# Attention probabilities transposed on VectorE, value products in four 32-row strips of TensorE, in a fused encoder layer

## The chip, the cores and the metric

The program runs on one core of one Trainium2 chip. Its time is the device time of that core in microseconds. Shown are the median of three timed runs and one execution taken by the hardware profiler. TensorE (PE), VectorE (DVE), ScalarE (ACT), GpSimd (POOL) and SyncE (SP, which here only issues DMAs) each work through their own list of instructions in order, and wait for each other by semaphores.

## The reference

One encoder layer on x of 512 positions by 1024 channels, in float32:

```python
x = x + 0.5 * swiglu(rms_norm(x, ffn1_norm), ffn1_w_gate, ffn1_w_up, ffn1_w_down)   # D_FF = 2752
h = rms_norm(x, mix_norm)
u = h @ w_in                       # 512 Fourier | q 8x64 | k 2x64 | v 2x64
f_out = fourier_mixer(u[..., :512], fnet_w, fnet_b)      # 4 groups of 128
a_out = gqa_attention(...)         # per-head rms_norm of q and k, axial rotary, then for each head
    scores = q_blk @ k.T * 64**-0.5                      # 8 heads x 4 blocks of 128 queries, 512 keys
    p = jax.nn.softmax(scores, axis=-1); out = p @ v
x = x + concat([f_out, a_out]) @ w_out
x = x + 0.5 * swiglu(rms_norm(x, ffn2_norm), ...)
y = rms_norm(x, final_norm)
```

## The kernel before

The layer runs in three stretches: the first feed-forward block (to about 340 us), the mixer with the Fourier part, the attention and the output projection (about 340 to 497 us), and the second feed-forward block with the ending. The change is in the mixer. Numbers are kept to float32 accuracy by splitting each operand into a high part, rounded to the type fp32r that TensorE multiplies in one pass, and a low part, the rest; a product is then three products (`product`, L163 to L166: high by high, high by low, low by high), accumulated in a PSUM bank of 128 x 512 float32. The high part is a copy on ACT (or on DVE for the names in `HI_DVE`), the low part a subtraction on DVE (`lows`, L123).

The mixer's work is cut into named steps, each a small function put into the dictionary `ops`. A long table, `ORDER`, names them in the order in which they are recorded, and so fixes the order on every engine. The eight PSUM banks go round through a list: a step that writes takes the first spare bank (`bank_for`), the last step that reads it gives it back (`read`). The steps to follow are, for a pair of heads t (0 to 3), a key/value head b (0 or 1) and a block of 128 queries c (0 to 3):

- `n1.c`, `n1.m`, `n1.p`: column sums of squares of the mixer's input, and its reciprocal root r on GpSimd; `n1.t` and `n1.b` turn r into a row on PE and copy it. `k.s0`, `s1`, `s2` and the same for q0 to q3 make the scales of the heads, `sc`; `kw`, `kp`, `km` bring those of k onto k.
- `s` (L1188, L1189): the scores of 128 queries by 512 keys, two products of 512 columns.
- `m` (L1194, L1195): the row's maximum on DVE, then times the scale. `e` (L1202): the exponential on ACT, which also gives the row's sum z.
- `t` (L1214): for each block of 128 keys, four transposes of 128 x 128 on PE, which bring the probabilities of four query blocks into one bank, keys down the partitions. `h` (L1219) copies that bank to its high part `ph` on ACT, `l` subtracts it to `pl` on DVE.
- `v` (L1257): the value products. The 128 stationary columns in `vst` hold the high and the low part of v beside each other (64 + 64), so two products of 512 columns, by `ph` and by `pl`, do for a key block; after four key blocks `o.c` (ACT) and `o.a` (DVE) add the two halves of the bank.
- `z.r`, `z.w`, `z.p`, `r.m`, `r.h`, `r.l`: the division by z and the split of the result for the output projection `y0` to `y7` (24 products of 512 columns each).

So there are 32 steps of each of `s`, `m`, `e`, `t`, `h`, `l` and `v`: 128 transposes and 64 value products.

Of the kernel before, what the change touches and what calls it, by code (L numbers as in the profile page):

```python
# [37 lines left out]
HI_DVE = ("f0", "f1")  # L38
# [5 lines left out]
wk.r wq0.r wv.r cos wk.h wk.l wq0.h k.0 k.1 k.2 k.3 k.4 wv.h k.5 wq0.l k.6 wq1.r k.7 k.sq q0.0 wq1.h n1.c  # L44
k.rc n1.m k.sw n1.p q0.1 q0.2 q0.3 q0.4 wq1.l q0.5 wq2.r n1.t q0.6 q0.7 wq2.h q1.0 k.rs k.pq wv.l q0.sw
n1.b v.0 v.1 k.s0 k.s1 wq2.l q0.rc f2.r wq3.r q0.rs q0.ah q0.bh k.s2 v.2 kw v.3 v.4 v.5 v.6 q0.sq q0.al
q0.bl v.7 vt kp wq3.h km q1.1 wq3.l q0.pq f0.r q0.s0 k1.0 k0.0 k0.1 q1.2 q1.3 q1.4 q1.5 k1.2 k0.2 vp q1.6
q1.7 k0.3 s003 s001 s000 k1.1 k1.3 s010 f1.r v0.h v0.l q0.s1 q0.s2 f0.h m001 m003 s002 q1.sw m002 m010 q1.sq
q1.sd q1.pq e002 m000 v1.h e000 e001 e003 q2.0 q2.1 q2.2 q1.s0 q1.s1 f0.l q1.rc q1.rs v1.l q2.3 q2.4 q1.bh
q2.5 q2.6 q2.7 q2.sw t001 e010 f1.h f1.l q2.rc t000 q3.0 s012 h000 l000 s011 m011 t002 h002 h001 m012 q1.ah  # L50
q1.al q2.sq q3.1 q3.2 q3.3 q3.4 q3.5 q3.6 q1.bl q3.7 s013 l002 e011 v000 e012 f2.h l001 v001 q2.sd q3.sw
q2.rs t003 m013 q2.ah q3.rc q3.sq v002 e013 q2.bh f2.l s100 q1.s2 m100 s102 h003 q3.sd e100 f00.0 t010 f3.r
q2.bl h010 q2.pq l003 q2.s0 q2.s1 t013 m102 e102 s101 m101 f00.1 f00.u q2.al v003 l010 e101 t011 h011 q3.rs
s103 t012 f02.0 h013 l011 z0.r o00.c o00.a q3.bh v010 v011 m103 h012 l012 q3.pq q3.s0 l013 e103 s110 m110
s201 q3.ah s111 q3.bl v012 v013 o01.c t100 m111 h100 l100 e111 o0.r t101 h101 t102 h102 o01.a fw.r f02.1
e110 s112 m112 e112 z0.w pos q2.s2 l102 f01.0 s113 l101 z0.p m113 e113 s203 r0.m f02.e s200 m200 v100 v101
t103 t110 f01.1 r0.h h103 l103 z1.r f02.h v102 f01.u e200 q3.al q3.s1 v103 o10.c t112 m201 h110 r0.l h112
s202 m202 l110 t113 m203 f03.0 f03.1 v110 f3.h q3.s2 o10.a e201 s210 f03.e f3.l t111 l112 f10.0 f02.l h113
h111 l111 e202 f10.1 f03.h e203 s211 v111 m210 o2.r fw.h e210 t200 h200 t202 l113 m211 v112 s300 l200 v113
h202 t201 f10.u h201 l202 o11.c s212 m212 e212 s213 z1.w e211 f12.0 fw.l l201 f12.1 m300 e300 m213 e213  # L60
o11.a z1.p r1.m s301 v200 t203 r1.h f03.l h203 f12.e l203 f12.h z2.r z2.w v201 v202 t211 s302 m302 t210 h210
l210 s303 m303 h211 l211 v203 o20.c o20.a t212 h212 m301 f11.0 f13.0 e302 s311 l212 f12.l o0.h o0.l r1.l
t213 f11.1 f11.u m311 v210 v211 f13.1 h213 l213 f13.e e303 v212 s310 d00 m310 e301 t302 o1.r o1.h o1.l t301
f13.h f13.l e310 v213 o21.c t300 o21.a h302 l302 map0 map0.h map0.l d10 h300 l300 map1 z2.p d00.h map1.h
d00.l e311 t303 r2.m map1.l h303 l303 v300 s312 h301 m312 d20 d01 o2.h s313 d11 l301 v301 v302 v303 m313
e312 d01.h d01.l c0.s o2.l e313 t312 d11.h d11.l o30.c d31 o30.a h312 l312 o4.r c0.c c0.q c0.o t311 d10.h
# [1544 lines left out]
```

## Time and profile before

| | us |
|---|---|
| median of three runs | 838.54 (837.89 to 838.76) |
| the profiled execution's own time | 837.96 |
| its span, first to last instruction | 836.2 |
| PE busy | 829.4, 99% |
| DVE, ACT, POOL busy | 603.4, 461.9, 62.5 |

The span is 1.8 us shorter than the execution's own time, and that execution lies 0.6 us under the median. The busy time of PE is the union of matmuls that overlap one another: a matmul's duration holds its way through the array, and the next one starts long before it ends. What a matmul costs PE is therefore read from the distance between starts.

### The profile page before, as it was taken

To read this page: it belongs to the slowest core of one execution; us is meant where nothing else is said; L and a number is where in the kernel's file an instruction comes from. 1 tells how busy PE (TensorE), PEld (TensorE's weight loads), DVE (VectorE), ACT (ScalarE), POOL (GpSimd) and SP (SyncE) were. 2 spreads that over 40 slices of the span, in tenths; PEclk is the share of its full clock that TensorE was granted. 3 is DMA by queue.
4 is the path that set the end of the run, shared out by engine and by line. 5 is a ranking of instruction groups with operands and counts; after the bars stand their busy time and mean duration, and the time that the engine had idled before them with its cause. 6 is when DMAs were issued, how large, how long until landed. Compare 5 with 4: busy or idle time off the path is not lost.

```text
span 836.2 us, 13649 instructions
## 1 busy us (share of the span) xinstructions
PE 829.4 (99%) x5418; PEld 752.3 (90%) x5418; DVE 603.4 (72%) x923; ACT 461.9 (55%) x770; POOL 62.5 (7%) x69
## 2 busy tenths in 40 slices
PE   9999999999999999999999999999999999999997
PEld 7888998899989998889999888899988999899986
DVE  7977884578656867699999478878755885578563
ACT  7654763366434644677776446546533663356452
POOL 0111000000000000222000000110000000000001
PEclk9999999999999999999999999999999999999999
DMA  7787765468365423414020326777554674456122
GB/s 253 189 199 191 199 187 147 117 159 226 97 169 151 121 58 114 151 51 146 26 76 26 100 57 170 187 182 197 165 154 125 179 206 131 116 167 189 45 78 101
DMA packets 46110, 117.16 MB, mean 140 GB/s; under 512 B 5216, under 2 KB 9952, under 8 KB 45920
## 3 DMA queue, kind: packets, MB, share of 16 engines
q1 hardware_dynamic: 38128, 92.57, 33.5%
q0 software_dynamic: 7648, 23.47, 16.4%
q8 instruction: 42, 0.69, 0.3%
q10 hardware_dynamic: 272, 0.26, 0.1%
q14 instruction: 20, 0.16, 0.1%
HBM read 111.83 MB, written 2.10 MB: 136 GB/s over the span
## 4 chain that ended last, share of the span: by engine, by line
PE 99%; issue 0%; DVE 0%; POOLq 0%; POOL 0%; ACT 0%
PE r L429 23%; PE q L429 11%; PE dn L166 9%; PE dn L164 9%; PE dn L165 9%; PE p L429 6%; PE mix L164 4%; PE mix L166 3%; PE mix L165 3%; PE gu L766 3%; PE gu L164 3%; PE gu L165 3%; PE gu L166 3%; PE mix L1257 2%; PE mix L1214 2%; PE mix L1188 1%
## 5 line engine op out<-in xcount | busy, mean ns | idle before, releaser
L429 PE MATMUL r<-rt,ring 128*128 128x256 f32 x1686 | 204.9, 276 | 0.0
L429 PEld LDWEIGHTS r<-rt,ring 128*128 128x128 f32 x1686 | 198.5, 188 | 0.9
L165 PE MATMUL dn<-at,ring 128*128 128x512 f32 x295 | 114.8, 389 | 0.0
L166 PE MATMUL dn<-at,ring 128*128 128x512 f32 x295 | 114.8, 389 | 0.0
L164 PE MATMUL dn<-at,ring 128*128 128x512 f32 x295 | 114.8, 389 | 0.0
L429 PE MATMUL q<-rt,ring 128*128 128x256 f32 x840 | 106.6, 276 | 0.0
L374 ACT CAST ring<-s 128x1024 fp32r<-128x1024 f32 x70 | 73.5, 1050 | 58.3 <-DVE s L394 51.5
L581 DVE SCALAR_TENSOR_TENSOR gx<-dn,gx 128x512 f32<-128x512 f32 x61 | 42.1, 691 | 81.1 <-PE dn L166 81.1
L429 PEld LDWEIGHTS q<-rt,ring 128*128 128x128 f32 x840 | 100.4, 188 | 0.0
L123 DVE TENSOR_TENSOR ring<-s,ring 128x1024 fp32r<-128x1024 f32 x70 | 85.3, 1219 | 0.6 <-ACT ring L374 0.6
L156 ACT CAST ring<-raw_dn 128x768 fp32r<-128x768 f32 (+2 forms) x48 | 40.7, 852 | 75.6 <-PE dn L165 70.5
L166 PEld LDWEIGHTS dn<-at,ring 128*128 128x128 f32 x295 | 55.4, 188 | 11.5
L165 PEld LDWEIGHTS dn<-at,ring 128*128 128x128 f32 x295 | 55.4, 188 | 11.1
L164 PEld LDWEIGHTS dn<-at,ring 128*128 128x128 f32 x295 | 55.4, 188 | 11.0
L346 POOL DMA_DIRECT2D s<-in_wgu x35 | 30.1, 861 | 423.5 <-DVE ring L123 146.7
L429 PE MATMUL p<-rt,ring 128*128 128x256 f32 x420 | 53.3, 276 | 0.0
L123 DVE TENSOR_TENSOR ring<-raw_dn,ring 128x768 fp32r<-128x768 f32 (+2 forms) x48 | 46.7, 977 | 7.1 <-ACT ring L156 7.1
L429 PEld LDWEIGHTS p<-rt,ring 128*128 128x128 f32 x420 | 50.2, 188 | 0.0
L123 DVE TENSOR_TENSOR ring<-raw_g,ring 128x1024 fp32r<-128x1024 f32 x35 | 42.6, 1217 | 0.0
L123 DVE TENSOR_TENSOR at<-u,at 128x512 fp32r<-128x512 f32 x35 | 24.2, 693 | 20.3 <-ACT at L484 20.2
L472 DVE TENSOR_TENSOR u<-g,u 128x512 f32<-128x512 f32 x35 | 24.0, 687 | 19.8 <-ACT u L469 19.8
L374 ACT CAST ring<-raw_g 128x1024 fp32r<-128x1024 f32 x35 | 36.8, 1051 | 0.0
(312 smaller groups left out, 1523.0 us busy)
## 6 DMA issues: line engine op xcount, KB each, us to landing
s<-in_wgu SPq DMA_DIRECT2D x70, 256.0 KB, 4.2
s<-in_wgu POOLq DMA_DIRECT2D x35, 512.0 KB, 5.7
raw_g<-in_wgu SPq DMA_DIRECT2D x35, 512.0 KB, 4.0
raw_dn<-in_wd SPq DMA_DIRECT2D x44, 384.0 KB, 3.9
raw_u<-in_wgu SPq DMA_DIRECT2D x35, 256.0 KB, 4.1
raw_gu<-in_wgu SPq DMA_DIRECT2D x12, 512.0 KB, 3.5
raw_o<-in_wo SPq DMA_DIRECT2D x8, 512.0 KB, 3.6
raw_dn<-in_wd SPq DMA_DIRECT2D x5, 448.0 KB, 4.2
```

What stands on the lines that cost most here:

```text
L123: nc.vector.tensor_tensor(out=lo, in0=src, in1=asf(hi), op=ALU.subtract)
L156: nc.scalar.copy(hi[:, :n, :], raw[:, :n, :])
L164: nc.tensor.matmul(ps, whi, mhi, start=first, stop=False)
L165: nc.tensor.matmul(ps, whi, mlo, start=False, stop=False)
L166: nc.tensor.matmul(ps, wlo, mhi, start=False, stop=last)
L346: nc.gpsimd.dma_start(out=blocks(t), in_=up, accum_op=ALU.add)
L374: nc.scalar.copy(ts[0], src)
L429: nc.tensor.matmul(ps[:, c], a[:, ks], b[:, i, c], start=first and i == 0 and o == 0, stop=i == KH - 1 and o == 2, skip_group_check=not fi ...
L472: nc.vector.tensor_tensor(out=self["u"], in0=self["g"], in1=self["u"], op=ALU.mult)
L581: nc.vector.scalar_tensor_tensor(out=x[d][:, t], in0=ps[:, t], scalar=0.5, in1=x[d][:, t], op0=ALU.mult, op1=ALU.add)
L766: nc.tensor.matmul(pss[c], w[:, k % 2, c], m[k], start=k == 0 and m is hh and w is hi, stop=k == KD - 1 and w is lo,)
L1214: nc.tensor.transpose(pts[n][:, c * P : (c + 1) * P], prob[t, b, c][:, kc * P : (kc + 1) * P], ident)
```

## The change

It changes six things, all in the mixer.

1. The probabilities are transposed by DVE (`x`, L1245: `nc.vector.transpose` of 128 x 512, in blocks of 32 x 32), from SBUF to SBUF. There is no `t` on PE any more. `h` copies the result to the high half of a tile `its`, `l` subtracts to the low half.
2. After that, a strip of 32 partitions holds the probabilities of its own 32 queries of a block: down the strip 32 keys, and along it, for each of 16 groups of keys, the 32 queries. So the value products work strip by strip: `p` (L1261) takes eight query blocks of one key/value head at once, and for each of 16 groups of 32 keys and each of high and low gives four matmuls, one for each strip, into four different banks: 128 rounds of four over the four sets `p0` to `p3`, 512 matmuls of 32 rows by 256 columns. For this all of v must stand in each of the four strips: `vr` (L1053) copies it there by 32 small DMAs from GpSimd's queue. `o.c` and `o.a` gather the result from four banks in pieces of 64 x 128.
3. `m` is one instruction (L1227): it scales the scores in place in PSUM by minus the head's scale, and gives the row's minimum beside it; `e` then takes the exponential of minus the scores.
4. The head scales: `s0` works in PSUM, `s2` moves from DVE to GpSimd, with `rr` (r squared) and `rq` made there in `n1.p`. The row of r (`n1.t`, `n1.b`) is gone; v gets r after its transposes (`vm`).
5. Low parts move from DVE to GpSimd by a list, `LOWS_POOL`: 27 of the 32 `l` steps, and the low parts of eight weights of 128 x 1024 and of fw. High parts of seven tiles move to DVE (`HI_DVE`), those of f0 and f1 back to ACT; `z.w` moves from GpSimd to ACT.
6. `ORDER` is another table; some tiles share memory.

```diff
-HI_DVE = ("f0", "f1")
+LOWS_POOL = """
+000 001 003 010 011 012 013 100 101 102 103 110 111 113 200 201 202 203 211 212 213 300 301 302 303 311 312 f0 fw o0
+o1 o2 o4 o5 o6 wq3
+""".split()
+HI_DVE = """
+003 203 o3 o5 o6 wq2 wv
+""".split()
 ORDER = """
-wk.r wq0.r wv.r cos wk.h wk.l wq0.h k.0 k.1 k.2 k.3 k.4 wv.h k.5 wq0.l k.6 wq1.r k.7 k.sq q0.0 wq1.h n1.c
+wk.r wq0.r wv.r cos wk.h wk.l wq0.h k.0 k.1 k.2 k.3 k.4 wv.h k.5 wq0.l k.6 wq1.r k.7 k.sq q0.0 wq1.h n1.c k.pq n1.m
...
-    def lows(lo, src, hi):
-        nc.vector.tensor_tensor(out=lo, in0=src, in1=asf(hi), op=ALU.subtract)
+    def lows(lo, src, hi, by=None):
+        (by or nc.vector).tensor_tensor(out=lo, in0=src, in1=asf(hi), op=ALU.subtract)
...
             def _():
                 pq = banks[f"pq{name}"][:, 0:8].rearrange("p (c t) -> p c t", t=2)
-                nc.vector.tensor_tensor(out=v, in0=pq, in1=rx, op=ALU.mult)
+                nc.vector.tensor_tensor(out=pq, in0=pq, in1=rr.unsqueeze(2).to_broadcast([P, 4, 2]), op=ALU.mult)
+                nc.vector.tensor_scalar(out=v, in0=pq, scalar1=1.0 / HD, scalar2=EPS, op0=ALU.mult, op1=ALU.add)
                 read(f"pq{name}")
-                nc.vector.tensor_tensor(out=v, in0=v, in1=rx, op=ALU.mult)
-                nc.vector.tensor_scalar(out=v, in0=v, scalar1=1.0 / HD, scalar2=EPS, op0=ALU.mult, op1=ALU.add)
...
-                nc.vector.scalar_tensor_tensor(out=v, in0=v, scalar=factor, in1=rx, op0=ALU.mult, op1=ALU.mult)
+                nc.gpsimd.tensor_tensor(out=v, in0=v, in1=factor.unsqueeze(2).to_broadcast([P, 4, 2]), op=ALU.mult)
...
+            def spread(a):
+                for i in range(4):
+                    src, dst = slice(32 * i, 32 * i + 32), slice(32 * a, 32 * a + 32)
+                    nc.gpsimd.dma_start(
+                        out=vrep[dst].rearrange("p (c i) e -> p c i e", i=4)[:, :, i],
+                        in_=stage[v][src].rearrange("p c o e -> p c (o e)"),
+                    )
...
-                nc.vector.tensor_reduce(out=mx, in_=sps[n], axis=AX.X, op=ALU.max, negate=True)
-                nc.vector.tensor_tensor(out=mx, in0=mx, in1=f, op=ALU.mult)
+                nc.vector.tensor_scalar(
+                    out=sps[n], in0=sps[n], scalar1=f, scalar2=None, op0=ALU.mult, op1=ALU.min, accum_out=mx
+                )
...
+                nc.vector.transpose(turned[n], probs[n])
+            op(f"h{n}")(lambda: (nc.vector.tensor_copy if n in HI_DVE else nc.scalar.copy)(ph, turned[n]))
+            op(f"l{n}")(lambda: lows(pl, turned[n], ph, nc.gpsimd if n in LOWS_POOL else nc.vector))
...
+            @op(f"p{st}")
+            def _():
+                held[f"p{st}"] = [[spare.pop(0) for _ in range(4)], 4]
+                sets[st] = held[f"p{st}"][0]
+                for j in range(16):
+                    for o in range(2):
+                        for a in range(4):
+                            rows = slice(32 * a, 32 * a + 32)
+                            nc.tensor.matmul(
+                                sets[st][a][:, : 8 * 32], vrep[rows, j], its[rows, o, :, 32 * j : 32 * j + 32],
+                                start=j == 0 and o == 0, stop=j == 15 and o == 1, skip_group_check=True,
+                            )
...
+                for a in range(4):
+                    nc.scalar.copy(out_of(t, a), part(slice(HD, P), t, a))
...
+                for a in range(4):
+                    nc.vector.tensor_tensor(out=out_of(t, a), in0=part(slice(0, HD), t, a), in1=out_of(t, a), op=ALU.add)
...
-                for c in range(4):
-                    nc.tensor.transpose(pts[n][:, c * P : (c + 1) * P], prob[t, b, c][:, kc * P : (kc + 1) * P], ident)
...
-                for i, p in enumerate(parts[n]):
-                    nc.tensor.matmul(outs[t, b], w, p, start=kc == 0 and i == 0, stop=kc == 3 and i == 1)
```

What moves, engine by engine. On PE, in the middle of the attention, before (L1188 and L1189 are scores, L1214 transposes of the probabilities e, L1257 value products by the high and low parts ph and pl):

```order
L1188 MATMUL mix6_3415<-ks10_3420,qb0_3557 128x512
L1189 MATMUL mix6_3415<-ks11_3421,qb0_3557 128x512
L1257 MATMUL mix1_3410<-ph000_3747,vst_3422 128x512
L1257 MATMUL mix1_3410<-pl000_3749,vst_3422 128x512
L1257 MATMUL mix1_3410<-ph001_3762,vst_3422 128x512
L1257 MATMUL mix1_3410<-pl001_3805,vst_3422 128x512
L1214 MATMUL mix4_3413<-ident_108,e000_3683 128x128
L1214 MATMUL mix4_3413<-ident_108,e001_3685 128x128
L1214 MATMUL mix4_3413<-ident_108,e002_3677 128x128
L1214 MATMUL mix4_3413<-ident_108,e003_3687 128x128
```

There they stand in small groups among other products. On PE at the start of `p0`, now (L1092 to L1094 are the Fourier projection; its holds the transposed probabilities, vrep v in four strips):

```order
L1092 MATMUL mix0_3402<-ring_61 128x256
L1093 MATMUL mix0_3402<-ring_61 128x256
L1094 MATMUL mix0_3402<-ring_61 128x256
L1261 MATMUL mix3_3405<-its_3415,vrep_3417 128x256
L1261 MATMUL mix5_3407<-its_3415,vrep_3417 128x256
L1261 MATMUL mix6_3408<-its_3415,vrep_3417 128x256
L1261 MATMUL mix4_3406<-its_3415,vrep_3417 128x256
```

The four last rows are one round: four strips, four banks. 32 such rounds follow on each other without anything between, four times in the mixer, and the transposes are gone.

On DVE at the end of the mixer, before (L1300 adds an output chunk to x, L191 is the low part of the next block's input, L1311 adds up its squares in acc2, and the L123 rows are low parts of weights of the second feed-forward block):

```order
L1300 TENSOR_TENSOR gx_69<-mix6_3415,gx_69 128x512
L123 TENSOR_TENSOR ring_61<-raw_gu2_0_5046,ring_61 128x1024
L1300 TENSOR_TENSOR gx_69<-mix0_3409,gx_69 128x512
L191 SCALAR_TENSOR_TENSOR ring_61<-gx_69,ring_61 128x512 x4
L1311 TENSOR_TENSOR acc2_3390<-acc2_3390,sq2_5_0_5010 128x512
L1300 TENSOR_TENSOR gx_69<-mix4_3413,gx_69 128x512
L1311 TENSOR_TENSOR acc2_3390<-acc2_3390,sq2_6_0_4993 128x512
L123 TENSOR_TENSOR ring_61<-raw_gu2_1_5082,ring_61 128x1024
L123 TENSOR_TENSOR at2_5043<-raw_gu2_42_5117,at2_5043 128x1024
L1311 TENSOR_TENSOR acc2_3390<-acc2_3390,sq2_7_0_5021 128x512
```

And now (the same steps are L1328, L203, L1341 and L131; mix1 is the last output chunk):

```order
L1328 TENSOR_TENSOR gx_69<-mix7_3409,gx_69 128x512
L131 TENSOR_TENSOR ring_61<-raw_gu2_0_5404,ring_61 128x1024
L1341 TENSOR_TENSOR acc2_5266<-acc2_5266,sq2_5_0_5357 128x512
L203 SCALAR_TENSOR_TENSOR ring_61<-gx_69,ring_61 128x512 x2
L1341 TENSOR_TENSOR acc2_5266<-acc2_5266,sq2_4_0_5344 128x512
L203 SCALAR_TENSOR_TENSOR ring_61<-gx_69,ring_61 128x512
L1328 TENSOR_TENSOR gx_69<-mix1_3403,gx_69 128x512
L203 SCALAR_TENSOR_TENSOR ring_61<-gx_69,ring_61 128x512
L131 TENSOR_TENSOR ring_61<-raw_gu2_1_5440,ring_61 128x1024
L131 TENSOR_TENSOR at2_5401<-raw_gu2_42_5475,at2_5401 128x1024
L203 SCALAR_TENSOR_TENSOR ring_61<-gx_69,ring_61 128x512
L1341 TENSOR_TENSOR acc2_5266<-acc2_5266,sq2_6_0_5380 128x512
```

One L1341 more, of the last chunk, follows. Of the ten steps that DVE did ahead of the last output chunk or behind it, more stand behind the last two chunks now. PE reads acc2 after the first 21 products of the next block in both (L219 before, L231 now).

On GpSimd at the start of the mixer, before (L233 and L949 are reciprocal roots, L1239 the sums z made wide, L1369 loads of the Fourier tables):

```order
L233 TENSOR_TENSOR r1_91<-ms1_92,mhalf_117 128x4
L949 TENSOR_TENSOR sc_3407<-sc_3407,mhalf_117 128x4x2 x4
L1239 COPY zw0_4047<-z0_3676 128x512
L1369 DMA chan_3404<-in_chan 128x512
L1369 DMA pos_3405<-in_pos 128x2056
L1369 DMA odd_3406<-in_odd 128x258
L949 TENSOR_TENSOR sc_3407<-sc_3407,mhalf_117 128x4x2
L1239 COPY zw1_4297<-z1_3852 128x512
```

And now (L959 are the same roots, L963 the products `s2`, L131 low parts, L1053 the copies of v):

```order
L245 TENSOR_TENSOR r1_91<-ms1_92,mhalf_117 128x4
L1387 TENSOR_TENSOR rr_3439<-r1_91 128x4
L1388 TENSOR_SCALAR rq_3440<-r1_91 128x4
L959 TENSOR_TENSOR sc0_3434<-sc0_3434,mhalf_117 128x8
L963 TENSOR_TENSOR sc0_3434<-sc0_3434,r1_91 128x8
L959 TENSOR_TENSOR sc1_3435<-sc1_3435,mhalf_117 128x8
L963 TENSOR_TENSOR sc1_3435<-sc1_3435,rq_3440 128x8
L131 TENSOR_TENSOR more_3400<-raw_wq3_3612,more_3400 128x1024
L131 TENSOR_TENSOR ring_61<-raw_f0_3660,ring_61 128x1024
L959 TENSOR_TENSOR sc2_3436<-sc2_3436,mhalf_117 128x8
L1053 DMA vrep_3417<-its_3415 32x4x128 x4
```

Where GpSimd had 13 instructions from `n1.p` to the last of the mixer, it now has 84: 36 low parts, 32 copies of v, and the roots, scales and table loads, in one queue behind each other.

283 lines of the change are left out of this document (141 added, 142 removed).

## The prediction

> **What bounds the kernel now.** I read the page first, then the stages, then the starts of the matmuls one by one. On the page stand TensorE's busy share and the chain that ended last:
>
> ```profile
> PE 829.4 (99%) x5418; PEld 752.3 (90%) x5418; DVE 603.4 (72%) x923; ACT 461.9 (55%) x770; POOL 62.5 (7%) x69
> PE 99%; issue 0%; DVE 0%; POOLq 0%; POOL 0%; ACT 0%
> ```
>
> PE is the bound: the chain never leaves it. So a gain must come out of PE's own work, and a loss from new work or from a wait on PE. The stages of the mixer (columns: busy time of PE, weight loads, DVE, ACT, POOL, then the granted clock, DMA share and GB/s):
>
> ```profile
> 380.00:420.00 40.00, 40.00 (x291) 36.71 (x290) 37.34 (x82) 31.20 (x66) 6.58 (x7) 1.00 0.30 94
> 420.00:460.00 40.00, 40.00 (x270) 36.27 (x269) 37.45 (x77) 28.85 (x62) 1.23 (x2) 1.00 0.14 49
> 340.00:500.00 160.00, 160.00 (x940) 139.81 (x939) 130.99 (x250) 106.20 (x199) 16.94 (x13) 1.00 0.23 76
> ```
>
> PE is full and at full clock (1.00). In the attention, 380 to 460 us, DVE is at 74.8 of 80 us, so it stands close behind PE; over the whole mixer it has 29 us to spare, and GpSimd (POOL) is almost idle. Next, PE's starts in the middle of the attention:
>
> ```profile
> 428.31 0.60 PE L1214 MATMUL mix<-ident,e 128*128 128x128 f32 x4
> 428.66 0.36 PE L1063 MATMUL mix<-ring 128*128 128x256 f32 x1
> 428.86 0.28 PE L1064 MATMUL mix<-ring 128*128 128x256 f32 x1
> 428.98 0.28 PE L1065 MATMUL mix<-ring 128*128 128x256 f32 x1
> ...
> 430.16 0.40 PE L1257 MATMUL mix<-ph,vst 128*128 128x512 f32 x1
> ...
> 431.09 0.28 PE L1063 MATMUL mix<-ring 128*128 128x256 f32 x1
> ```
>
> Ten products of 256 columns stand between 428.98 and 430.16: 0.118 us each. Four value products of 512 columns take 430.16 to 431.09: 0.2325 us each. Four transposes and the product behind them take 428.31 to 428.86, 0.55 us; less 0.12 for that product, a `t` costs 0.43 us, with the delay that it puts on its successor.
>
> **What PE loses.** 32 `t` by 0.43 = 13.8 us; 64 value products by 0.2325 = 14.9; the row of r (`n1.t`), four transposes, 0.4. Together 29.1 us, all of it on the path.
>
> **What PE gains, the disputed term.** 512 matmuls of 32 rows by 256 columns, in 128 rounds of four strips. The trace before has no matmul of fewer rows, so I bound a round from both sides. If the four strips run beside each other, a round is one product of 256 columns, 0.118 us: 15.1 us in all. If each runs alone, four of them, 0.47 us: 60.4 us. What could keep them apart is the weight load, of which each matmul has one. Its price, where the matmul is too short to hide it:
>
> ```profile
> 341.75 0.95 PE L219 MATMUL mix<-ones,acc 128*128 128x2 f32 x8
> 342.56 0.49 PE L164 MATMUL mix<-ring 128*128 128x512 f32 x1
> 342.88 0.40 PE L165 MATMUL mix<-ring 128*128 128x512 f32 x1
> ```
>
> Eight matmuls of 2 columns take 0.81 us, and the product behind them starts its successor 0.32 us later, not 0.227: 0.101 to 0.113 us each, all of it weight load. Four in a row would be 0.40 to 0.45 us a round. The Trainium skill speaks on both sides here. "TensorE: Matmul & The Clock Gate", section on LDWEIGHTS, says that a load of 32 rows takes as long as one of 128, since the columns count: that speaks against the change, and no row here has a 32-row load to agree or not. The same page, Part 3 on packing small matmuls, says that loads for another strip are pulled ahead of running matmuls, and gives 3.07 times for four strips at 512 columns; by that figure a round would be, as an estimate, 4 x 0.118 / 3.07 = 0.154 us, 19.7 in all. No run here shows either. I take 0.14 us a round, near the row of one product since the strips have rows and banks of their own, with 0.02 for not starting at once: 17.9 us. PE's own work then falls by 29.1 - 17.9 = 11.2 us.
>
> **What DVE, ACT and GpSimd do to it.** The groups concerned (mean ns, and busy us ahead of it):
>
> ```profile
> L1194 DVE TENSOR_REDUCE mx<-mix 128x1 f32<-128x512 f32 x32 | 21.8, 682 | 1.2 <-PE mix L1189 1.1
> L123 DVE TENSOR_TENSOR pl<-mix,ph 128x512 fp32r<-128x512 f32 x32 | 21.7, 685 | 0.9 <-ACT ph L1219 0.6
> L123 DVE TENSOR_TENSOR ring<-raw_o,ring 128x1024 fp32r<-128x1024 f32 x5 | 6.1, 1224 | 4.9 <-ACT ring L858 4.9
> L1272 DVE TENSOR_TENSOR oo<-mix,oo 64x512 f32<-64x512 f32 x8 | 5.4, 674 | 0.4 <-ACT oo L1267 0.3
> L1195 DVE TENSOR_TENSOR mx<-mx,sc 128x1 f32<-128x1 f32 x32 | 5.1, 160 | 1.1
> L1390 POOL TENSOR_TENSOR gx<-gx,rb 128x256 f32<-128x256 f32 x2 | 1.5, 744 | 2.4 <-ACT rb L246 2.4
> L1174 ACT CAST eh<-fo 128x512 fp32r<-128x512 f32 x4 | 2.5, 628 | 2.6 <-DVE fo L1171 2.6
> ```
>
> DVE loses 21.8 + 5.1 (maxima), 21.7 (low parts), 5.4 (sums of halves), eight low parts of 1.22 and one of 0.69: 64.5 us. It gets 32 transposes and 32 scalings with minimum. No row shows either. A transpose reads and writes as much as a subtraction: I take 0.69 us; its lower end is that too, since no DVE row of this size is quicker than 0.67, its upper end twice that. The scaling lies between 0.68 (one pass) and 0.84 (and the small multiply's 0.16 to read out the minimum). With five low parts of 0.69, 32 sums of 64 x 128 at about 0.27 (between 0.16 for one element and 0.67 for 512) and some 3 us of high parts: 22 + 22 to 27 + 3.4 + 8.6 + 3 = 59 to 64 us. So DVE keeps its load; with dear transposes it gets 22 us more. ACT reads its 30 copies from SBUF at 0.63 and gets 32 small copies for 8 larger ones and `z.w`: 5 us more by such rows, on 106 of 160.
>
> GpSimd gets 36 low parts. Twice the 0.744 us of its 128 x 256 row is 1.49 us for 512 columns, an upper end as fixed parts count double: 28 x 1.4 and 8 x 2.8, 62 us. Its queue otherwise:
>
> ```profile
> 384.88 1.64 POOL L949 TENSOR_TENSOR sc<-sc,mhalf 128x8 f32<-128x8 f32 x1 [14.88 <-DVE sc L945]
> 391.19 0.55 POOL L1369 DMA_DIRECT2D pos<-in_pos  x1
> 403.07 1.03 POOL L1239 COPY zw<-z 128x512 f32<-128x512 f32 x1 [9.04 <-DVE z L1234]
> 424.00 0.62 POOL L1239 COPY zw<-z 128x512 f32<-128x512 f32 x1 [19.89 <-DVE z L1234]
> 402.94 0.68 DVE L123 TENSOR_TENSOR qa<-rot_q,qa 64x512 fp32r<-64x512 f32 x1
> ```
>
> 32 copies of v at 0.55 are 17.6 us, roots and scales some 12: about 92 us, in the 110 us between the first scores and `p3`. That is cover, but thin. It also waits for DVE: the copy at 403.07 took 0.41 us longer than the one at 424.00, and DVE was in a subtraction of two SBUF operands until 403.62. The Trainium skill ("SBUF — State Buffer", on who interferes with whom) has GpSimd's reads share a port with DVE's second SBUF input, held for a whole instruction. The trace agrees, 1.03 against 0.62.
>
> **New waits on PE.** Two places can be counted. First, the sums of squares at the end of the mixer. DVE's rows there:
>
> ```profile
> 488.22 0.68 DVE L1311 TENSOR_TENSOR acc<-acc,sq 128x512 f32<-128x512 f32 x1
> 488.82 0.74 DVE L191 SCALAR_TENSOR_TENSOR ring<-gx,ring 128x512 fp32r<-128x512 f32 x1
> 489.49 0.68 DVE L1300 TENSOR_TENSOR gx<-mix,gx 128x512 f32<-128x512 f32 x1
> ...
> 498.80 1.22 DVE L123 TENSOR_TENSOR ring<-raw_gu,ring 128x1024 fp32r<-128x1024 f32 x1
> 499.93 1.22 DVE L123 TENSOR_TENSOR at<-raw_gu,at 128x1024 fp32r<-128x1024 f32 x1
> 501.07 0.69 DVE L1311 TENSOR_TENSOR acc<-acc,sq 128x512 f32<-128x512 f32 x1
> 502.15 0.95 PE L219 MATMUL ss<-ones,acc 128*128 128x2 f32 x8
> ```
>
> Steps of 512 take 0.60 or 0.67 from start to start, of 1024 1.13. Before, the last sum ended at 501.76, 0.4 us ahead of its reader. In the new order DVE has, from the third-last output chunk's addition on, seven steps of 0.60, six of 0.67 and three of 1.13, 11.6 us, and starts 0.4 us after that chunk's last product did; PE has 43 products of 0.227 from there to L231, 9.8 us. PE waits about 2.3 us. Second, the scale of k: `kp` now stands only 33 products and `pq` behind the sums of `n1.c`, and its chain has a second GpSimd step (`s2`) behind the 1.6 us root. Before:
>
> ```profile
> 342.82 2.76 ACT L900 ACTIVATE sw_k<-mix,qkg 32x512 f32<-32x512 f32 x4
> 355.01 0.60 PE L993 MATMUL mix<-ident,kw 128*128 128x128 f32 x4
> ```
>
> Now PE is there at 342.56 + 0.9 + 33 x 0.227 = 350.9. DVE comes to `s0` behind k's rotation, which waits for L900 until 345.6, and two low parts: 345.6 + 0.67 + 2 x 1.13 = 348.5; 0.3 for `s0`, 1.64 for the root, 0.16 to 0.55 for `s2`, 0.5 for `kw`, handovers 0.1 each: 351.5 to 352. A wait of 0.9. Further, each set enters and leaves the strips: eight changes, by the 0.1 us that a `t` puts on its successor, 0.8 us. Between, with DVE, ACT and GpSimd as full as above, I put 2 us, 0 to 6.
>
> **The sum.** -11.2 + 2.3 + 0.9 + 0.8 + 2 = -5.2 us. Against the profiled execution, 837.96, that is 832.8 us; the median lies 0.6 above it, so I say 833.3. With rounds of 0.118 and none of the 2 us it is 828.5 in the median; with 0.16 (twice that 0.02 for late starts) and the 6 us, 840.
>
> **Rivals.** *The loads follow on each other* (slower): the strips' matmuls start only as their weights are in, one after another. For it: PE takes its instructions in order, and L219 shows 0.101 to 0.113 us a load. Against: strips have separate rows. 512 x 0.101 to 0.113 = 51.7 to 57.9 us, less 29.1, with the 3.2 us of the counted waits: 864 to 871 by the median. It decides from (29.1 - 6) / 128 = 0.18 us a round. *Two at a time*: 256 x 0.118 = 30.2, so +1.1, and 6 of waits: 845, give or take 3. *DVE or GpSimd becomes the bound*: transposes at 1.4 us give DVE 22 us more where it had 5 to spare in 80; or GpSimd's 36 low parts each wait 0.4 us as at 403.07, 14 us on its 92, and the sets wait. Either takes away the gain and some 6 to 14 us more: 838 to 852. *That the change does not do what it says* is the first rival's upper case: strips not used at all, 60.4 us, 873.
>
> **How the numbers follow.** Forecast 0.52, loads in a row 0.22, two at a time 0.10, DVE or GpSimd 0.16. The forecast's own range is 828 to 840. The other cases at 838 to 852 bring what is covered to 0.78, so the range must reach the quick end of the first rival: 828 to 865. A measurement tells 0.2%, 1.7 us. Faster by more: 0.46, nearly all of the forecast; within: 0.07, its slow end and the quickest of the DVE case; slower: 0.47.
>
> **What would show it.** L1261's rounds: starts of the same strip 0.12 to 0.16 us apart if I am right, 0.24 if two go together, over 0.4 if loads queue; then I am wrong whatever else holds. A DVE transpose of 0.69 us and a scaling under 0.85; GpSimd's subtraction near 1.4; PE waiting about 2 us ahead of L231, about 1 ahead of L1001, and little ahead of L1261.

## Result and the profile after

Twelve runs of the changed kernel have a median of 839.05 us (835.62 to 841.71), twelve of the kernel before 838.28 (837.84 to 838.76): ratio 1.0006, 95% interval 0.9992 to 1.0020. No change in the median is measured, where 833.3 was forecast; but the new runs spread over 6 us and the old ones over 0.9. The profiled execution is the quickest of the twelve: 835.62, its span 833.8, TensorE at full clock until its work ends.

Of the page after, TensorE's busy time and the chain that ended last; the chain now leaves PE:

```profile
PE 820.3 (98%) x5734; PEld 742.3 (89%) x5734; DVE 600.1 (72%) x938; ACT 458.2 (55%) x793; POOL 134.2 (16%) x140
PE 89%; DVE 6%; ACT 2%; issue 1%; DMA 1%; POOL 0%; SPq 0%; POOLq 0%; DVEq 0%; ACTq 0%
```

The stages of the mixer (columns as in the prediction):

```profile
340.00:380.00 40.00, 39.77 (x207) 33.62 (x206) 30.32 (x56) 26.10 (x45) 21.64 (x25) 1.00 0.39 103
380.00:440.00 60.00, 56.10 (x597) 50.67 (x600) 59.01 (x136) 48.66 (x119) 51.37 (x52) 1.00 0.45 108
440.00:500.00 60.00, 57.54 (x476) 48.10 (x468) 40.44 (x78) 28.88 (x61) 15.61 (x9) 1.00 0.25 75
```

Before, PE was busy for the whole of each of these stages (40.00, 60.00 and 60.00 us); now 3.9 us are missing from 380 to 440, where DVE has 59.01 of 60, and 2.5 at the end. The waits of PE in the mixer (us in total, times, longest):

```profile
PE ss L231 <- DVE acc L1341: 2.5, 1, 2.5
PE mix L172 <- ACT e L1236: 1.1, 2, 0.6
PE mix L1221 <- DVE qa L131: 1.0, 1, 1.0
PE mix L1221 <- ACT e L1236: 0.7, 1, 0.7
PE mix L1221 <- DVE oo L1281: 0.6, 1, 0.6
PE mix L172 <- ACT fq L1190: 0.3, 1, 0.3
PE mix L1001 <- DVE kw L995: 0.2, 1, 0.2
```

And the new operations, by groups; then, from the timeline, one set of rounds and the product behind it (start, us, and so on):

```profile
L131 POOL TENSOR_TENSOR its<-x,its 128x512 fp32r<-128x512 f32 x27 | 37.6, 1418 | 7.8 <-ACT its L1247 6.4 <-DVE its L1247 1.4
L1227 DVE TENSOR_SCALAR_CACHE_REDUCE mix<-mix,sc 128x512 f32<-128x512 f32 x32 | 23.1, 743 | 2.0 <-PE mix L1222 1.2 <-POOL sc L963 0.7
L1245 DVE STREAM_TRANSPOSE x<-e 128x512 f32<-128x512 f32 x32 | 21.7, 692 | 0.0
L1261 PE MATMUL mix<-its,vrep 32*128 32x256 f32 x512 | 16.9, 283 | 0.0
L1261 PEld LDWEIGHTS mix<-its,vrep 32*128 32x128 f32 x512 | 16.1, 184 | 1.2 <-ACT e L1236 0.4 <-issue 0.4 <-ACT qa L1309 0.4
```

```profile
397.08 4.33 PE L1261 MATMUL mix<-its,vrep 32*128 32x256 f32 x128
401.35 0.50 PE L1221 MATMUL mix<-ks,qb 128*128 128x512 f32 x1
```

From its first start to the next product this set takes 401.35 - 397.08 = 4.27 us; the four take 4.27, 4.05, 4.21 and 4.14, 16.67 in all, 0.130 us a round. One product of 256 columns took 0.118: the four strips do run beside each other. From sums to sums (L219 before, L231 after) the mixer went from 502.15 - 341.75 = 160.40 us to 499.65 - 342.03 = 157.62. That is a gain of 2.8 us at full clock. What took it back, and the spread, is the subject of the experiments.

### The profile page after: what moved, and what is told of

Same layout as the page of the kernel before. It is cut to its first block, busy times and chain, and to the rows that moved or that the text cites. A ratio compares the mean times of both kernels' runs of the same rounds, so it can differ in the third digit from the quotient of the medians.

```text
span 833.8 us, 14442 instructions
## 1 busy us (share of the span) xinstructions
PE 820.3 (98%) x5734; PEld 742.3 (89%) x5734; DVE 600.1 (72%) x938; ACT 458.2 (55%) x793; POOL 134.2 (16%) x140
## 4 chain that ended last, share of the span: by engine, by line
PE 89%; DVE 6%; ACT 2%; issue 1%; DMA 1%; POOL 0%; SPq 0%; POOLq 0%; DVEq 0%; ACTq 0%
PE r L441 23%; PE q L441 11%; PE dn L174 9%; PE dn L173 9%; PE dn L172 9%; PE p L441 6%; PE mix L172 3%; PE gu L172 2%; PE gu L173 2%; PE mix L174 2%; PE mix L173 2%; PE gu L174 2%; PE gu L778 2%; PE mix L1261 1%; DVE mix L1227 1%
## 5 line engine op out<-in xcount | busy, mean ns | idle before, releaser
L131 DVE TENSOR_TENSOR ring<-s,ring 128x1024 fp32r<-128x1024 f32 x70 | 85.3, 1219 | 0.6 <-ACT ring L386 0.6
L131 DVE TENSOR_TENSOR ring<-raw_dn,ring 128x768 fp32r<-128x768 f32 (+2 forms) x48 | 46.7, 977 | 7.4 <-ACT ring L164 7.4
L131 DVE TENSOR_TENSOR ring<-raw_g,ring 128x1024 fp32r<-128x1024 f32 x35 | 42.6, 1217 | 0.0
L131 POOL TENSOR_TENSOR its<-x,its 128x512 fp32r<-128x512 f32 x27 | 37.6, 1418 | 7.8 <-ACT its L1247 6.4
L131 DVE TENSOR_TENSOR at<-u,at 128x512 fp32r<-128x512 f32 x35 | 24.2, 692 | 20.2 <-ACT at L496 20.2
```

What stands on the lines that cost most here:

```text
L131: (by or nc.vector).tensor_tensor(out=lo, in0=src, in1=asf(hi), op=ALU.subtract)
```

## Experiments

Times are medians, with the lowest and highest run behind them; the kernel before, run beside each of these kernels, had 838.3 to 838.5.

### What lowers the clock?

In the twelve runs a lower mean clock goes, by and large, with a longer time (0.998 at 835.6, 0.990 at 841.7). Three kernels separate the suspects, the strips and the work that GpSimd got; a fourth repeats the change.

> The changed kernel once more, nothing altered, for more times and another profile. Its twelve runs lay between 835.6 and 841.7 us, with the mean granted clock from 0.998 down to 0.990, while those of the kernel before stayed within 837.8 and 838.8; the one profiled execution, 835.6, had the full clock until TensorE's work ended. Theory one (the strips): the clock falls where four strips of TensorE run at once; then a profile with a mean clock under 0.997 shows the granted clock under 1.00 in or right behind the four sets, at 397, 416, 439 and 453 us, and nowhere before 390. Theory two (the company): it falls because GpSimd now works beside the other engines; then the low clock begins with GpSimd's low parts, from 360 us on. Theory three (the chip): another program's load on the same chip, and this kernel before shows the same scatter in this call. Both of the first two expect 836 to 842 here, median 838 to 840, and the kernel before within 1 us.

Measured 839.08 (837.40 to 842.03), ratio 1.0012, interval 1.0002 to 1.0022. This profile had a mean clock of 0.990 and shows where (the stretch and its length, PE busy, loads, DVE, ACT, POOL, then the clock):

```profile
380.21:383.63 3.42, 2.08 (x19) 2.00 (x18) 3.38 (x9) 1.14 (x3) 1.22 (x2) 1.00 0.64 144
383.63:387.04 3.41, 2.25 (x8) 2.05 (x9) 3.28 (x8) 2.85 (x5) 3.33 (x7) 0.50 0.86 282
387.04:390.45 3.41, 3.41 (x18) 3.41 (x17) 3.32 (x3) 0.62 (x1) 3.41 (x2) 0.50 0.25 38
390.45:393.87 3.42, 3.42 (x28) 3.24 (x27) 2.97 (x4) 2.99 (x6) 0.73 (x2) 1.00 0.10 16
...
499.67:503.09 3.42, 0.96 (x5) 0.50 (x4) 3.15 (x5) 0.07 (x1) 0.00 (x0) 1.00 0.54 190
503.09:506.50 3.41, 3.41 (x13) 3.02 (x14) 0.16 (x1) 0.65 (x1) 1.04 (x1) 0.50 0.33 117
506.50:509.92 3.42, 3.42 (x10) 2.54 (x9) 1.84 (x3) 2.58 (x4) 0.00 (x0) 0.50 0.20 20
509.92:513.33 3.41, 3.41 (x19) 2.88 (x18) 2.85 (x5) 2.64 (x4) 0.00 (x0) 1.00 0.77 273
```

The clock is 1.00 or exactly 0.50, it changes only every 3.41 us, and it falls right behind a stretch in which PE waited: for the low part of q at 382 us and for the sums at 500 us, ahead of the first set and behind the last. Neither of the first two theories put it there, and against the third the kernel before, run beside it, stayed within 837.8 and 838.8. At half clock a product of 512 columns starts 0.43 us after the one before it (506.89, 507.32, 507.75 us), where it is 0.227 at full clock. So a half-clock stretch that PE streams through costs 3.41 x (1 - 0.227 / 0.43) = 1.6 us, and here there are four, the first of them with a wait in it.

> The four 32-row matmuls of a round are replaced by one of 128 rows by the same 256 columns; banks, waits, order and all other engines stay. It leaves out that each strip's queries are kept apart (sums over the strips are written). TensorE then has 128 matmuls of 0.118 us in the sets in place of 128 rounds of 0.125 to 0.131 (read from the changed kernel's trace), 1.0 to 1.5 us less in all. The strips: the clock stays at 0.998 or more in all runs, they agree within 1.2 us, and the median is 834 to 835. The company: the clock falls as often as in the changed kernel, scatter 4 us or more, median 836.5 to 839.

```diff
-for a in range(4):
-    rows = slice(32 * a, 32 * a + 32)
-    nc.tensor.matmul(sets[st][a][:, : 8 * 32], vrep[rows, j], its[rows, o, :, 32 * j : 32 * j + 32], ...)
+nc.tensor.matmul(sets[st][j % 4][:, : 8 * 32], vrep[:, j], its[:, o, :, 32 * j : 32 * j + 32], ...)
```

Measured 839.17 (837.20 to 841.18), ratio 1.0009, interval 1.0000 to 1.0018, clocks 0.991 to 0.996; the profile has half clocks at 384 and 500 us. The sets took 16.0 us in place of 16.7, 0.7 less where 1.0 to 1.5 was put, and the median is no lower than the change's. The clock falls without strips: they are not the cause.

> Each set's 32 rounds are run twice into the same banks (so the sums come out doubled). Price of a round if it is the same beside the profile's waits: 128 x 0.128 = 16.4 us more at full clock, less up to 2 us of waits that the longer sets hide: 850 to 852 at full clock. The strips: the time at a lowered clock doubles too, mean clock down to 0.98 to 0.99, median 855 to 860, scatter over 6 us. The company: no lower clock than the changed kernel's, median 852 to 856.

```diff
-for j in range(16):
+for n, j in enumerate([*range(16), *range(16)]):
...
-start=j == 0 and o == 0, stop=j == 15 and o == 1, ...
+start=n == 0 and o == 0, stop=n == 31 and o == 1, ...
```

Measured 854.75 (853.80 to 855.69), ratio 1.0194, interval 1.0181 to 1.0207: 15.7 us more than the change, with a clock of 0.992 to 0.994, no lower than the change's. The sets of 64 rounds last 7.7 to 7.9 us from first to last start where those of 32 lasted 3.85 to 4.06, 15.1 us more for 128 rounds: 0.118 us each, one product of 256 columns. What a round costs beyond that is paid once a set.

> All 36 low parts that the change gives to GpSimd go back to VectorE: 28 x 0.60 + 8 x 1.13 = 25.8 us more on an engine that had 160 - 130 = 30 us idle in the mixer, but at most 3 in the 80 us of the attention; of them some 22 us fall into that stretch. So PE waits longer there: 850 to 862 at full clock under every theory. The strips: the clock still falls in most runs, scatter of some us. The company: the clock is at 0.998 or more in all runs, which agree within 1.2 us.

```diff
-LOWS_POOL = """000 001 003 ... wq3""".split()
+LOWS_POOL = ()
```

Measured 862.44 (859.69 to 863.64), ratio 1.0289, interval 1.0276 to 1.0302, clocks 0.983 to 0.988. GpSimd's busy time from 340 to 500 us falls from 88.6 to 31.5 us (the copies of v stay with it) and the clock is lower still: its low parts are not the cause. The sets now wait for low parts from DVE, 6.8 us in four waits, and the profile has three falls of the clock, each behind waits of PE.

### Is it the pauses of TensorE?

A fourth theory came from these rows: a pause, not the work, lowers the clock. If so, the kernel before must show it when it is made to wait, and the changed kernel must lose it without its waits.

> The kernel before, with nothing of the change, but five more instructions on VectorE (acc = max(acc, acc), 0.60 us each) ahead of the last sum of squares, so that the sums on TensorE wait about 3.0 - 0.4 = 2.6 us at 502 us. Pauses: this kernel now shows the changed kernel's scatter too: a half clock of 3.4 or 6.8 us right behind 502 us in most runs, 0 to 3.4 us of TensorE's time, so 841 to 844.5 with a median about 843. The strips, or GpSimd's company, or the transposes as the cause of the lower clock: 838.4 + 2.6 = 841.0, all runs within 1.2 us, clock 0.998 or more.

```diff
+for _ in range(5 if d == KD - 1 else 0):
+    nc.vector.tensor_tensor(out=n2.acc, in0=n2.acc, in1=n2.acc, op=ALU.max)
 nc.vector.tensor_tensor(out=n2.acc, in0=n2.acc, in1=sqs[name], op=ALU.add)
```

Measured 843.31 (842.95 to 844.82), ratio 1.0064, interval 1.0051 to 1.0077, clocks 0.994 to 0.996: 4.9 us more for a wait of 3.1, where the wait alone would make 841.5. A half-clock stretch is 1.6 of the rest. The row of the sums, and the stretches around it:

```profile
505.51 1.05 PE L219 MATMUL ss<-ones,acc 128*128 128x2 f32 x8 [3.07 <-DVE acc L1314]
```

```profile
500.31:503.73 3.42, 2.13 (x10) 1.43 (x8) 3.35 (x5) 0.33 (x1) 0.00 (x0) 1.00 0.60 176
503.73:507.14 3.41, 1.63 (x11) 1.54 (x12) 2.42 (x5) 0.00 (x0) 0.29 (x1) 1.00 0.40 131
507.14:510.55 3.41, 3.41 (x9) 2.65 (x9) 1.29 (x2) 3.11 (x4) 0.71 (x1) 0.50 0.00 0
510.55:513.97 3.42, 3.42 (x18) 2.81 (x18) 3.09 (x4) 2.57 (x4) 0.00 (x0) 1.00 0.72 220
```

> The kernel before with two more instructions on VectorE ahead of the last sum of squares instead of five: TensorE waits about 2 x 0.60 - 0.4 = 0.8 us at 502 us where the other waited 3.2. Pauses with a threshold at about 0.4 of a stretch of 3.41 us: eight 2-column matmuls (0.8 us, nothing streamed) and 0.8 us of wait leave 1.8 / 3.41 = 0.53 even if they fall into one stretch, so the clock stays: median 838.4 + 0.8 = 839.2, all runs within 1.2 us, clock 0.998 or more. If any pause on TensorE could lower the clock: 840 to 842 with a scatter of over 2 us.

```diff
-for _ in range(5 if d == KD - 1 else 0):
+for _ in range(2 if d == KD - 1 else 0):
```

Measured 839.61 (838.87 to 840.83), ratio 1.0017, interval 1.0008 to 1.0026; the clock is 0.997 or more in every run. The runs spread over 2.0 us where 1.2 was put, at full clock; why, no run shows. Here the same place has

```profile
504.12 1.05 PE L219 MATMUL ss<-ones,acc 128*128 128x2 f32 x8 [0.90 <-DVE acc L1314]
```

```profile
501.80:505.20 3.40, 2.50 (x16) 1.93 (x15) 2.83 (x4) 0.00 (x0) 0.00 (x0) 1.00 0.73 227
505.20:508.60 3.40, 3.40 (x18) 2.79 (x19) 1.46 (x3) 2.55 (x4) 1.01 (x1) 1.00 0.20 82
```

So not any pause does it. In the profiled stretches of the changed kernel, at 382 and 497 us, the clock stayed:

```profile
379.62:383.03 3.41, 2.39 (x23) 2.31 (x21) 3.31 (x10) 2.30 (x5) 2.84 (x4) 1.00 0.56 120
...
495.67:499.08 3.41, 1.51 (x7) 0.94 (x5) 3.38 (x5) 0.71 (x2) 0.00 (x0) 1.00 0.51 136
499.08:502.50 3.42, 2.85 (x17) 2.52 (x18) 0.71 (x3) 1.18 (x2) 1.04 (x1) 1.00 0.49 171
```

With the eight 2-column matmuls, about 1.0 us of busy time, taken off where they lie in the stretch, PE streamed 0.33 (380.21 in the repeat), 0.28 (499.67) and 0.17 (503.73) of it ahead of a fall, and 0.42 (379.62), 0.43 (501.80), 0.44 (495.67) and more where none came. They can't count in full: 2.08 us busy with them was followed by a fall, 1.51 without them was not.

The other profiles can be asked the same. Count for each matmul only the time from its start to the next start that its columns take: 0.227 us for 512 columns at full clock, 0.43 at half clock, almost nothing for two columns. From 5 us on until TensorE's work ends, the 17 profiles of this case have 17 full-clock stretches that are followed by a fall, and PE streamed 0.06 to 0.37 of each; in the 4037 others it streamed 0.40 or more (the nearest pair: 0.37 at 379.6 us in the kernel with doubled rounds, 0.40 at 495.67 in the changed kernel). The same count says how long a fall lasts: of 26 half-clock stretches, the nine that were streamed for 0.70 or less were followed by another, the 17 with 0.91 or more by full clock.

The grid lies differently in each execution, so the wait of 2.5 us falls into one stretch or is shared by two: the same kernel has the loss or not. The Trainium skill, "TensorE: Matmul & The Clock Gate", Part 1, has a free-running window of 3413 ns and a clock at half or full: the rows agree. The same page of the Trainium skill, in its section on oscillation, has the rule of thumb that no gap should be longer than some 3.4 us; here waits of 2.5 us were enough, and in a kernel below one of 1.65, and the measurement decides.

> The changed kernel with one step of TensorE's list moved: the sums of squares at the end of the mixer (L231), which waited 2.5 us for VectorE, stand 12 more products of 512 columns later (ahead of the fourth k of the second gate product), the row of r 12 products later too. Theory four (pauses): the granted clock is set anew every 3.41 us from how much TensorE streamed in that stretch, and falls to half where less than some 0.4 of it was streamed; of the two places where this is seen, 382 us and 500 us, one is taken away. Then: 2.5 us of wait gone and about half of the 3.4 us by which the changed kernel's median lies above its full-clock run: median 834.5 to 835.5, between 833 and 837, and a half clock at about 383 us only. Without that theory (the wait alone): 839.1 - 2.5 = 836.6, with the scatter of 836 to 842 less 2.5 as before, and half-clock stretches still at 500 us.

```diff
-[[gate(0, {KD - 1: column}), gate(1, {3: row})]]
+[[gate(0), gate(1, {3: column, KD - 1: row})]]
```

Measured 836.15 (834.07 to 837.51), ratio 0.9972, interval 0.9963 to 0.9980, clocks 0.995 to 0.998; the one half clock in the profile is at 385 us. 2.9 us better than the change, of which the wait is 2.5, less a new one of 0.8 for a low part of x that the sums' wait had covered; I put the rest down to the clock. The median alone doesn't decide: it lies between the two forecasts (834.5 to 835.5, and 836.6). What speaks for the pauses is that no half clock is left at 500 us, and that the runs spread over 3.4 us where those of the change spread over 6.1.

> The changed kernel with the other place alone: the score step that waited 1.0 us for the low part of q at 382 us (behind eight 2-column matmuls) is put behind the 12 Fourier products of 256 columns that followed it. Pauses: 1.0 us of wait gone and the half clock at 383 us with it: median 836 to 837, between 834.5 and 838.5, a half clock only at about 500 us. The wait alone: 838.1, and half-clock stretches at 383 us in most runs.

```diff
-q2.al s200 f03.0
+q2.al f03.0 s200
```

Measured 839.34 (835.55 to 841.89), ratio 1.0007, interval 0.9994 to 1.0020. The median is a miss: the wait of 1.0 us is still there behind the 12 products, another of 0.8 came up at 393 us, and the runs spread over 6.3 us. The half clocks, at 501 us only, are where the theory of the pauses had them.

> Both moves together. Pauses: no half clock before TensorE's work ends, runs within 1.2 us as in the kernel before, median 835.6 - 2.5 - 1.0 = 832.1, give or take 0.7. The waits alone, with the clock falling for another reason: 839.1 - 3.5 = 835.6, and a scatter of 4 us or more.

The two edits above together.

Measured 835.24 (834.00 to 836.87), ratio 0.9963, interval 0.9951 to 0.9975. No half clock before the end, clock 0.998 to 1.000 in all five runs: as the pauses have it. But the level is 3 us higher than forecast, and the spread 2.9 us where 1.2 was put: another cause of spread is left.

### What holds TensorE between 380 and 440 us?

DVE is full there. But its own instructions are longer at times. In the changed kernel's trace:

```profile
377.24 1.66 POOL L1053 DMA_DIRECT2D vrep<-its  x3
377.71 1.65 DVE L936 TENSOR_TENSOR rot_q<-rot_q,sw_q 128x512 f32<-128x512 f32 x1
...
386.67 2.00 DVE L131 TENSOR_TENSOR qa<-rot_q,qa 64x512 fp32r<-64x512 f32 x1
386.84 1.28 POOL L131 TENSOR_TENSOR its<-x,its 128x512 fp32r<-128x512 f32 x1
388.71 1.23 DVE L131 TENSOR_TENSOR more<-raw_f,more 128x1024 fp32r<-128x1024 f32 x1
388.85 2.23 POOL L131 TENSOR_TENSOR its<-x,its 128x512 fp32r<-128x512 f32 x1 [0.72 <-ACT its L1247]
```

The first two DVE rows have 0.69 us elsewhere, GpSimd's 2.23 has 1.28. I read the last four rows so: DVE's subtraction of 386.67 is held until GpSimd's low part ends at 388.12, GpSimd's of 388.85 until DVE's ends at 389.94. The Trainium skill's "SBUF — State Buffer", on who interferes with whom, has a lock held for a whole instruction by whichever of the two was first. The second pair agrees: DVE started 0.14 us ahead. The first pair doesn't show who was first: DVE's row starts 0.17 us ahead of the low part, while GpSimd was still in a root (385.20 to 386.87).

> The changed kernel with the 32 copies of v issued from SyncE's queue instead of GpSimd's (two weight loads there are put behind copies). In the changed kernel's trace VectorE's additions and subtractions of two SBUF operands took 1.65 us at 377.7 and 1.63 at 423.8, both while GpSimd was issuing these copies, where the same shapes take 0.69 and 0.64 elsewhere. Theory five (collisions: one of the two engines is held for as long as the other's instruction lasts): both return to under 0.80, GpSimd has 17.6 us less in its queue, and of TensorE's waits between 380 and 440 us (5 us beyond the ordinary distance of starts) 1.5 to 3 go, the wait at 382 us and its half clock most of all: median 835.5 to 837.5. The amount (VectorE is simply full there, 19.5 to 19.9 us in 20): the two instructions stay long or others become so, waits within 1 us of before, median 838.5 to 840.

```diff
-nc.gpsimd.dma_start(out=vrep[dst]..., in_=stage[v][src]...)
+nc.sync.dma_start(out=asf(vrep)[dst]..., in_=asf(stage[v])[src]...)
```

Measured 842.70 (838.77 to 843.42), ratio 1.0045, interval 1.0031 to 1.0060: slower, by my own doing. SyncE's queue took 0.6 to 0.7 us a copy, and the loads for q behind them came 5 us later than the 371.6 us of the changed kernel; PE then waited 2.8 us for q's low part at 385 us. Of the two instructions that should return to under 0.80, the addition did (0.69 at 381.26 us); the subtraction stayed at 1.63, at 427 us.

```profile
370.73 5.74 SPq L1053 DMA_DIRECT2D vrep<-its  x8
376.57 2.47 SPq L921 DMA_DIRECT2D sw_q<-early  x4
379.08 5.16 SPq L1053 DMA_DIRECT2D vrep<-its  x8
```

> The changed kernel with the later sums, the swap at 382 us and the copies of v on SyncE's queue together. Collisions and pauses together: no half clock before the end, waits between 380 and 440 us 1.5 to 3 us shorter than in the kernel with the first two moves (835.2): median 832.5 to 834, runs within 1.5 us. Pauses alone: 834.5 to 836, scatter 3 us as there.

The edits of the later sums, the swap and the copies together.

Measured 838.17 (837.73 to 839.04), ratio 1.0000, interval 0.9991 to 1.0008, with the same late loads. It has a half clock at 395 us where none was expected: the stretch ahead of it was streamed for 0.35, with a wait of 1.65 us for an exponential. The two kernels below put the copies behind the loads for q.

> The 27 low parts of the probabilities that GpSimd makes are left out, and the value products use the high parts twice (the output loses the low parts). GpSimd then has 37.6 us less. Collisions: VectorE's subtractions at 386.7 (2.00 us, beside a GpSimd low part from 386.84 to 388.13) and the like return to 0.70, TensorE's waits between 380 and 440 us fall by 1 to 2.5 us: median 836 to 838. The amount: VectorE's work is unchanged but for nothing, waits as before, median 838.5 to 840. If GpSimd's queue itself was late (its low parts awaited by the sets), the sets start earlier too; the changed kernel shows at most 0.3 us ahead of them.

```diff
-op(f"l{n}")(lambda: lows(pl, turned[n], ph, nc.gpsimd if n in LOWS_POOL else nc.vector))
+op(f"l{n}")(lambda: None if n in LOWS_POOL else lows(pl, turned[n], ph))
...
-its[rows, o, :, 32 * j : 32 * j + 32],
+its[rows, 0, :, 32 * j : 32 * j + 32],
```

Measured 835.41 (833.04 to 836.51), ratio 0.9961, interval 0.9949 to 0.9973: 3.6 us under the change. PE's waits (the 0.2 for k's scale left out):

```profile
PE ss L231 <- DVE acc L1341: 2.5, 1, 2.5
PE mix L1221 <- ACT e L1236: 0.7, 1, 0.7
PE mix L172 <- ACT e L1236: 0.5, 1, 0.5
PE mix L1221 <- DVE qa L131: 0.3, 1, 0.3
PE mix L172 <- ACT fq L1190: 0.3, 1, 0.3
```

Of the waits that the changed kernel has between the scale of k and the sums, 3.7 us, 1.8 are left, with the same instructions on DVE: half of them go with GpSimd's low parts. DVE's subtraction that took 2.00 us (386.67) takes 0.69 here (385.49). But GpSimd's queue is shorter too, so its copies and scales come earlier; the two are not told apart. The profile has a half clock behind the sums, at 496 us, and none at 382.

> The changed kernel with the copies of v on SyncE's queue once more, now behind the loads for q: four between the loads for q2 and q3, twelve behind the next weight load, all 16 of the second head ahead of a weight load that had stood before them. Collisions: VectorE's instructions at 377.7 and 423.8 (1.65 and 1.63 us) return to 0.70, and 1 to 2.5 us of TensorE's waits go: median 836.5 to 838. The amount: waits within 1 us of before, median 838.5 to 840. The loads for q are delayed by at most 1 us in either.

The copies as above, and in the order (`sd` are the loads for q):

```diff
-q2.sd q2.pq ... q3.sd x101 f3.r ... c2.s o4.r h013 ... d31.h vr1.2
+q2.sd vr0.1 q2.pq ... q3.sd x101 f3.r vr0.2 vr0.3 vr0.0 ... c2.s h013 ... d31.h vr1.2 o4.r
```

Measured 836.19 (835.14 to 838.40), ratio 0.9977, interval 0.9968 to 0.9986: 2.9 us under the change. DVE's addition for q and PE's wait behind it, in the repeat of the change:

```profile
378.63 2.54 DVE L936 TENSOR_TENSOR rot_q<-rot_q,sw_q 128x512 f32<-128x512 f32 x1
```

```profile
PE mix L1221 <- DVE qa L131: 2.5, 1, 2.5
```

On GpSimd, behind its copies, in that repeat:

```profile
379.28 1.33 POOL L131 TENSOR_TENSOR its<-x,its 128x512 fp32r<-128x512 f32 x1
```

And with the copies behind the loads:

```profile
378.09 0.69 DVE L936 TENSOR_TENSOR rot_q<-rot_q,sw_q 128x512 f32<-128x512 f32 x1
```

```profile
PE mix L1221 <- DVE qa L131: 0.5, 1, 0.5
```

One addition held for 1.65 us went with a wait of 1.0 (the changed kernel's profile), one for 2.54, or two for 1.61 and 1.68 (late sums), with 2.4 to 2.5, none with 0.5. So the wait at 382 us, and with it a fall of the clock, hangs on how DVE meets GpSimd. The copies are not the whole of it: the additions of 2.54 and of 1.68 us ended 0.56 us behind the low part that GpSimd starts after its copies (379.28 to 380.61 in the repeat, 379.09 to 380.43 with the late sums). In both kernels DVE had also stood idle for 0.5 us before, until the loads for q landed. Putting the copies elsewhere moves that low part too (here it starts at 375.14 us). And of the theory as put, half fell: the subtraction at 423 us stayed at 1.60 us, now beside a low part, and in other places DVE's additions ran in 0.69 beside copies. The later waits, 0.3 to 0.7 us each from 405 to 436 us, did not change: there it is DVE's amount, or was not told apart. The sums still wait 2.5 us, and the profile's one half clock is behind them, at 500 us.

> The same placing of the copies together with the later sums and the swap at 382 us. Collisions: 1 to 2 us under the kernel with those two moves (835.2): 833 to 834.3. The amount: 834.5 to 836.

These edits with the later sums and the swap.

Measured 833.56 (832.92 to 833.69), ratio 0.9941, interval 0.9929 to 0.9954: 4.7 us under the kernel before and 5.5 under the change, the best of all, with five runs within 0.8 us. No half clock before the end of TensorE's work; of the waits, 3.7 us are left.

> The kernel with the later sums and the swap, unchanged, a second time. If its spread of 834.0 to 836.9 came from the order in which VectorE and GpSimd happen to meet, the waits of TensorE between 380 and 440 us in this profile differ from those of the first (5.0 us) by as much as the time does, at a full clock; if from the clock, a half clock is seen. Median 834.5 to 836 either way.

Measured 834.35 (834.02 to 835.86), ratio 0.9953, interval 0.9940 to 0.9967. At full clock as before, with a span of 834.1 where the first profile had 832.2; one row differs most, that of scores waiting for exponentials, 1.6 us there and here

```profile
PE mix L1221 <- ACT e L1236: 2.5, 2, 1.8
```

All waits together came to 4.6 us there and 5.9 here, 1.3 of the 1.9 us between the two spans. So most of the rest of the spread lies in these waits; with the copies off GpSimd the runs agree within 0.8 us.

## Why the prediction was wrong

Two steps failed: the term "Between", put at 2 us, was 5.0; and the step from the profiled execution to the median, put at 0.6 us, was 3.4, since a wait can lower the clock behind it, and the prediction priced a wait at its length alone.

**Right.** PE's loss of work and the price of a round: rounds cost 0.130 us where 0.14 was put, and without the waits the mixer's own work fell by 10.8 us (160.40 - 157.62 = 2.8, and 8.0 of starts later than usual) where 11.2 less 0.8 was put. With the rounds as measured, 16.7 us, the prediction's own terms give 29.1 - 16.7 - 0.8 = 11.6; what the other 0.8 is, stays open. Loads in a row, two at a time, and unused strips are out. The transpose took 0.692 (0.69 forecast), GpSimd's low part 1.418 (1.4). The scaling took 0.743 and 0.135 for the reading, 0.88 together, a little over the 0.68 to 0.84. The wait for the sums was 2.5 to 2.6 (2.3), that for k's scale 0.2 to 0.4 (0.9).

**Mis-sized.** "Between, with DVE, ACT and GpSimd as full as above, I put 2 us, 0 to 6." The starts between 380 and 440 us are 5.0 us late. DVE came to 59 of 60 us, and it is the rival of DVE as the bound that happened in part: not by dear transposes, but, for some of it, by a handful of instructions held for about a microsecond where the two engines meet. Without GpSimd's low parts 1.9 of the 3.7 us of waits were gone, with the copies on SyncE's queue 0.5; the rest is DVE's amount or was not told apart. The prediction had quoted GpSimd being held by DVE (0.41 us) and not asked what the reverse does to an engine that is full. With these terms the sum is -10.8 + 2.6 + 0.4 + 5.0 = -2.8, so 835.2 at full clock; the profile has 835.62. This is no test of them, since the 10.8 was read from the same trace as what the waits leave.

**Missing.** The last 3.4 us, 835.6 to 839.05, are in no term of the sum. "the median lies 0.6 above it" carried over the spread of the kernel before, and each wait was priced at its own length. Before, PE never waited in the mixer and the clock was 1.00 in every row, so nothing there showed that a wait can cost more than it lasts. A stretch that PE streams for 0.37 or less puts the next one or two at half clock, 1.6 us each. Two such places, met or not, give up to 6.4 us, and the runs spread over 6.1. The four runs of the change at 839.05 to 839.15 us had mean clocks of 0.992 to 0.995 where the profiled one had 0.998. By that difference they spent 5 to 10 us more at half clock, an estimate of 2.4 to 4.7 us lost, so the clock can account for the 3.4. The wait at 382 us differs as well, 1.0 us in the changed kernel's profile and 2.5 in its repeat; runs without a profile don't show their waits, so the two are not told apart.

## What to carry to other kernels

Where an engine that has never paused is made to pause, price the pause and what follows it: on TensorE a wait of 2 to 3 us, or a shorter one beside matmuls of a few columns, may cost up to 3.2 us more, depending on the execution. A spread of runs that was not there before is a sign of it, and the granted clock in stretches of 3.41 us shows the place. When work moves to a near-idle engine, look at which instructions of a full engine it will stand beside, not only at its sum.

## Unexpected of the hardware

The granted clock took the values 1.00 and 0.50 alone, in steps of 3.41 us; the fall came after a stretch with 0.37 or less of it streamed, and never after one with 0.40 or more. A half-clock stretch was followed by another where 0.70 or less of it was streamed, by full clock from 0.91 on; none of the 26 lies between. 32-row loads took 184 ns, as long as the 188 of 128 rows, and four matmuls in strips still went through in the time of one. DVE additions of two SBUF operands took up to 2.54 us instead of 0.69 beside GpSimd's DMA issues and the low part behind them. One of 1.60 us, in the kernel without strips (377.66 to 379.26), lay beside issues alone (375.08 to 379.43). Others beside issues took 0.69; which ones hold it was not settled.
